# Normalising attention probabilities on GpSimd, with one reciprocal and one gate product per head

## The chip, the cores and the metric

One core of a Trainium2 chip runs the whole program in one launch. The metric is device microseconds, the median over several runs. The engines are named as in the profile: PE is TensorE (PEld its weight loads), DVE VectorE, ACT ScalarE, POOL GpSimd, SP the engine whose queue starts the transfers.

## The reference, cut to what matters

The reference is a decoder trunk of two layers on 512 tokens of width 1024. Each layer is a half-step SwiGLU, a mixer, and another half-step SwiGLU. The mixer projects the tokens into queries, keys and values, runs a pooling branch and an attention branch, and merges the two under gates. The part that the change touches is the softmax of two of the three attention branches and the gate that each is weighted with:

```python
def masked_softmax(s, mask):
    s = jnp.where(mask, s.astype(jnp.float32), -1e30)
    s = s - jnp.max(s, axis=-1, keepdims=True)
    p = jnp.where(mask, jnp.exp(s), 0.0)
    return p / jnp.maximum(jnp.sum(p, axis=-1, keepdims=True), 1e-30)
...
        return gc[..., 0:1] * o_cmp + gc[..., 1:2] * o_slc + gc[..., 2:3] * o_win
```

There are 16 heads of width 64 in two key groups. With 512 tokens the selected branch takes all blocks and the window spans the sequence, so both attend to every key up to the query.

## The kernel before

All activations stand transposed, features on the 128 partitions and the 512 tokens along the free axis. A float32 product is made of three passes over exact two-part splits of both operands (`mm3`, L114 to L116); each weight block is therefore split into `wh` on ACT (L107) and `wl` on DVE (L108) before PE can use it. Weights stream in through one queue (`load`, L92).

The program is a list of steps, but what the engines run is not in the order of the code: a scheduler places every instruction in its engine's queue, so that the products of one step stand between those of another. Each engine then works strictly through its own queue and waits by semaphores for the others.

In the attention stage of a layer, each of the 16 heads goes through two functions. `head_probs` makes, for each of four blocks of 128 queries (`qb`) and each of two branches (`br`), the scores on PE (L643 for the first two query blocks, L653 for the last two, in two banks `sc`), adds the distance and takes the minimum on DVE (L632, into a slot of `tbuf`; the scores are negated), takes the exponential and its row sum on ACT (L634, sums into the columns of `c`), and then on DVE inverts the sum (L658), multiplies it by the branch's gate (L659) and scales the block of probabilities by it (L662). A block of query `qb` has 128 (qb + 1) keys, so per head there are two blocks each of 128, 256, 384 and 512 columns. `head_out` of that head comes one step later in the code: it transposes the probabilities on PE (L675, 20 squares of 128 by 128 in six groups, three banks `pt`), splits each group into `ph` (ACT, L107) and `pl` (DVE, L108), and multiplies them with the values (L689, bank `pv`). The first group of a branch needs that branch's probabilities of all four query blocks.

Four times a layer `cmp_probs` makes the gated probabilities of the third branch for four heads; its scaling already runs on POOL (L605, tile `ec`). Between the heads stand the projections of the gates and of later queries (`ps_mm`, L114 to L116), which fill PE: `fill` in `mixer`. At the end of the mixer POOL also multiplies the pooling branch by its gate (L778, tile `bP`).

Of the kernel before, what the change touches and what calls it, by code (L numbers as in the profile page):

```python
# [14 lines left out]
ALU = mybir.AluOpType  # L15
# [3 lines left out]
T = 512  # L19
TB = T // P  # L20
# [9 lines left out]
MASKED = 1e30  # L30
# [21 lines left out]
class Trunk:  # L52
    """Activations are kept transposed: features on partitions, the 512 tokens
    along the free axis. A float32 product is three float32r passes over exact
    two-part splits of both operands (hi*hi + hi*lo + lo*hi)."""

# [10 lines left out]

# [1 line left out]
    def unit(self, tag, bufs, dt=F32, name=None, shape=(P, T)):  # L69
# [16 lines left out]

# [1 line left out]
    def load(self, src, kt, cols):  # L88
        """Rows (k p) of a [kt*128, cols] block onto partitions p."""
        raw = self.unit("wr", 3, F32, "wr", (P, 2048))  # L90
        v = raw[:, : kt * cols].rearrange("p (k c) -> p k c", k=kt)
        self.nc.sync.dma_start(v, src.rearrange("(k p) c -> p k c", p=P))  # L92
        return v

    def wsplit(self, v):
        """Exact split of a [128, a, b] weight block, a * b <= 1024."""
        a, b = v.shape[1], v.shape[2]
        out = []
        for nm in ("wh", "wl"):
            t = self.unit("w", 6, F32R, nm, (P, 1024))  # L100
            out.append(t[:, : a * b].rearrange("p (a b) -> p a b", a=a))
        hi, lo = out
        self.split(hi, lo, v)
        return hi, lo
# [5 lines left out]
    def mm3(self, out, terms, first=True, last=True):  # L110
        """out = sum over terms of lhsT^T rhs, each given as (lh, ll, rh, rl)."""
        n = len(terms)
        for i, (lh, ll, rh, rl) in enumerate(terms):
            self.nc.tensor.matmul(out, lh, rh, start=first and i == 0, stop=False)  # L114
            self.nc.tensor.matmul(out, lh, rl, start=False, stop=False)  # L115
            self.nc.tensor.matmul(out, ll, rh, start=False,  # L116
                                  stop=last and i == n - 1)

    def proj(self, tag, w, act):
        """One 128-feature output tile from a split weight unit."""  # L120
        out = self.bank(tag)
        hi, lo = w
        self.mm3(
            out,
            [(hi[:, k], lo[:, k], act[k][0], act[k][1]) for k in range(hi.shape[1])],
        )
        return out

# [1 line left out]
    def constants(self):  # L130
# [14 lines left out]
    def load_columns(self, names):  # L145
        """Per-feature vectors as columns, 128 features on partitions."""
        nc, io = self.nc, self.io
        rows = self.s("rows")[:, :P]
        r0 = min(ROWS[nm] for nm in names)
        n = 0  # L150
# [15 lines left out]
    def constants2(self):  # L166
        nc = self.nc

        def const(shape, name):
            return self.sb.tile(list(shape), F32, tag=name, name=name)  # L170

        # dist[p, c] = 384 + p - c, and MASKED where that is negative
        self.dist = const((P, T), "dist")
# [4 lines left out]
                                channel_multiplier=1)  # L178
        # distc[(j n), t] = t - (16 n + 31), and MASKED where that is negative
        self.distc = const((P, T), "distc")  # L180
        for j in range(4):
# [5 lines left out]
                                    channel_multiplier=-16)  # L187
        # qcol[(e d), m]: negated query scale over the slope of head 2 m + e
        self.qcol = const((P, ND), "qcol")
        for h in range(H):  # L190
            e = h % 2
            nc.gpsimd.memset(self.qcol[e * DH : e * DH + DH, h // 2 : h // 2 + 1],
                             -(DH ** -0.5) / SLOPES[h])
        # block[p, j] = 1 where p // 32 is j or j + 2
        self.block = const((P, 2), "block")
        nc.gpsimd.memset(self.block, 0.0)
        for j in range(4):
            nc.gpsimd.memset(self.block[32 * j : 32 * j + 32, j % 2 : j % 2 + 1], 1.0)
        # ramp[g, t] = w / (t + 1) for the first w tokens of pool group g
        self.ramp = const((P, 4, 16), "ramp")  # L200
# [4 lines left out]

# [1 line left out]
    def gain(self, x, col):  # L207
        """Split of x times its feature gain."""
        g = self.cols[:, col : col + 1]
        hi = self.unit("xg", 16, F32R, "xh")  # L210
        lo = self.unit("xg", 16, F32R, "xl")
        self.gained = (
            self.nc.scalar.activation(hi, x, AF.Copy, scale=g),
            self.nc.vector.scalar_tensor_tensor(lo, x, g, f32(hi), ALU.mult, ALU.subtract),
        )
        return hi, lo

    def norm_piece(self, d, x, row, split=True):
        """x[d] is final: gain it, split it, add its squares."""
        nc = self.nc  # L220
# [14 lines left out]
    def stats(self):  # L235
        """Per token 1/rms of the last normed activation, as columns per token
        block and (but after the last layer) along rows."""
        nc = self.nc
# [36 lines left out]

# [1 line left out]
    def run_steps(self, steps, nxt=0):  # L277
        """Steps are (fetch, run); each fetch is traced ahead of the run of the
        fetching step before it."""
        fetches = [i for i, (f, _) in enumerate(steps) if f]  # L280
        for i, (_, run) in enumerate(steps):
            while nxt < len(fetches) and (nxt == 0 or fetches[nxt - 1] <= i):
                steps[fetches[nxt]][0]()
                nxt += 1
            run()

    def units(self, src, n, kt, cols, cut, use, rows=False, pre=None):
        """Steps over n weight blocks [kt*128, cols], each cut into units of
        `cut` columns (or row tiles)."""
        steps = []  # L290
# [17 lines left out]

# [1 line left out]
    def ffn(self, wg, wu, wd, on_x):  # L310
# [41 lines left out]

# [1 line left out]
    def key_cmp_in(self, j, w):  # L354
        """Compressed-branch input as [(parity d), g, token pair]."""
        p = self.proj("mm", w, self.xg)
# [8 lines left out]
    def keys(self, br, w):  # L365
        """Keys stacked twice on partitions, hi and lo apart."""
        nc = self.nc
# [12 lines left out]
    def values(self, tb):  # L380
        """Values (stationary [keys, hi | lo]) and branch gates of a token block."""
        nc = self.nc
# [48 lines left out]
    def compress_steps(self, l, which):  # L431
        """MLP over the overlapping blocks of the compressed keys (which = 0) or
        values (1), the blocks stationary as [hi | lo]."""
        nc, io = self.nc, self.io
# [82 lines left out]

# [1 line left out]
    def pool_weights(self, l):  # L519
# [7 lines left out]
    def pool_unit(self, l, g, w):  # L527
        """Pool group g: trailing mean less the token, mixed and scaled."""
        nc = self.nc
# [28 lines left out]

# [1 line left out]
    def query_unit(self, m, w):  # L560
        """Per head of the pair the negated scaled query over the head's slope,
        [hi; lo] on partitions (odd heads [lo; hi])."""
        nc = self.nc
# [10 lines left out]
    def cmp_probs(self, qd):  # L574
        """Gated probabilities over the compressed keys of four heads, per head
        pair hi and lo stacked on partitions, [hi; lo] and [lo; hi]."""
        nc = self.nc
# [39 lines left out]
    def head_probs(self, h):  # L617
        """Gated probabilities of the selected and window branches, queries on
        partitions. The selection takes every block (8 of at most 16) and the
        window spans the sequence, so both attend to all keys up to the query."""  # L620
        nc = self.nc
# [15 lines left out]
        for qb in range(TB):  # L637
# [11 lines left out]
            else:  # L649
                for br in range(2):  # L650
# [5 lines left out]
                    probs[qb, br] = t  # L656
            ci = c[:, 2 * qb : 2 * qb + 2]
            nc.vector.reciprocal(ci, ci)  # L658
            nc.vector.tensor_mul(ci, ci, self.gates[:, qb, 3 * h + 1 : 3 * h + 3])  # L659
            for br in range(2):  # L660
                t = probs[qb, br]
                nc.vector.tensor_scalar(t, t, ci[:, br : br + 1], None, ALU.mult)  # L662

# [30 lines left out]

# [1 line left out]
    def mixer(self, l, on_x):  # L696
# [110 lines left out]

# [1 line left out]
    def run(self):  # L809
# [103 lines left out]
```

## Time and profile before

| | |
|---|---|
| median of 3 runs | 2415.21 us (2414.96 to 2421.27) |
| span of the profiled execution, first to last instruction | 2409.0 us |
| time outside the span, by the median | 6.2 us |
| busy: PE, DVE, ACT, POOL | 2377.3, 1398.9, 976.9, 51.5 us |
| attention stage of the first layer, of the second | about 490 to 765 us, 1655 to 1960 us |

The profile gives the span of its execution, not a device time of its own; the time outside the span is the difference to the median of the runs. A busy engine is not one at its peak: what a wait costs PE is read from the idle time of PE and PEld with what ended it, and from the distances between the starts of its products. In a row of grouped instructions, the form "out<-in xcount: min/median/max" or "busy us, mean ns" gives durations; "[idle before <-releaser]" in a timeline gives the wait ahead of a row.

### The profile page before, as it was taken

Reading aid. Unit: us, or ns where it says so; the run is one execution under the profiler, and the core shown is the slowest. Engines: PE = TensorE matmul, PEld = TensorE weight load, DVE = VectorE, ACT = ScalarE, POOL = GpSimd, SP = SyncE. Lnnn points to the kernel's source line nnn. Section 1 sums busy time; section 2 is a strip of 40 time slices with the busy share of each in tenths; the row PEclk is TensorE's granted clock in tenths of the full one; section 3 lists DMA queues with packets and bytes.
Section 4 is the critical chain, followed back from the end, with each engine's and each line's share of the span. In section 5 each row is a group of like instructions: output and inputs, shape, how many; then the busy total and the mean of one; then the engine's idle time right before and its main releaser. Section 6 shows DMA issues by size and latency. Waiting matters only on the chain.

```text
span 2409.0 us, 28552 instructions
## 1 busy us (share of the span) xinstructions
PE 2377.3 (99%) x11042; PEld 1951.9 (81%) x11042; DVE 1398.9 (58%) x2684; ACT 976.9 (41%) x1689; POOL 51.5 (2%) x106
## 2 busy tenths in 40 slices
PE   8999999999999999999999999999999999999998
PEld 6888888788888888888888888887888887888887
DVE  4434347778988544443544443567988975434444
ACT  4222234566666422222432222445666753222222
POOL 1000000000001000000000000000000010000000
PEclk9999999999999999999999999999999999999999
DMA  5332324422125422323232323335222253232321
GB/s 158 98 95 95 97 89 147 141 98 71 49 79 167 135 88 91 102 90 98 92 104 89 96 97 96 119 108 160 69 68 79 75 184 105 89 103 88 105 79 62
DMA packets 226007, 244.24 MB, mean 101 GB/s; under 512 B 8688, under 2 KB 206416, under 8 KB 225872
## 3 DMA queue, kind: packets, MB, share of 16 engines
q1 hardware_dynamic: 225696, 242.37, 31.6%
q8 instruction: 87, 1.43, 0.3%
q14 instruction: 48, 0.39, 0.1%
q10 hardware_dynamic: 176, 0.05, 0.0%
HBM read 223.53 MB, written 18.87 MB: 101 GB/s over the span
## 4 chain that ended last, share of the span: by engine, by line
PE 58%; issue 15%; DVE 1%; POOL 1%; DMA 1%; ACT 0%; POOLq 0%; DVEq 0%; SPq 0%; ACTq 0%
PE ps_mm L116 9%; PE ps_mm L115 9%; PE ps_mm L114 9%; PE ps_pv L689 4%; PE ps_sc L114 3%; PE ps_sc L115 3%; PE ps_sc L116 3%; PE ps_pt L114 3%; PE ps_pt L115 3%; PE ps_pt L116 3%; PE ps_pt L675 3%; PE ps_sc L653 2%; PE ps_sc L643 1%; DMA bP<-dB 1%; PE ps_sc L582 0%
## 5 line engine op out<-in xcount | busy, mean ns | idle before, releaser
L107 ACT ACTIVATE wh<-wr 128x1024 fp32r<-128x1024 f32 (+1 forms) x392 | 408.8, 1043 | 1099.5 <-PE ps_mm L115 414.3
L108 DVE TENSOR_TENSOR wl<-wr,wh 128x1024 fp32r<-128x1024 f32 (+1 forms) x392 | 469.9, 1200 | 76.6 <-ACT wh L107 75.5
L116 PE MATMUL ps_mm<-act,wl 128*128 128x512 f32 x704 | 280.8, 399 | 0.0
L114 PE MATMUL ps_sc<-xh,wh 128*128 128x512 f32 x704 | 277.1, 394 | 2.2 <-ACT x L838 2.2
L115 PE MATMUL ps_mm<-act,wh 128*128 128x512 f32 x704 | 277.6, 394 | 0.0
L114 PE MATMUL ps_mm<-act,wh 128*128 128x512 f32 x704 | 275.5, 392 | 0.0
L115 PE MATMUL ps_sc<-xl,wh 128*128 128x512 f32 x704 | 274.5, 390 | 0.0
L116 PE MATMUL ps_sc<-xh,wl 128*128 128x512 f32 x704 | 274.2, 389 | 0.0
L114 PE MATMUL ps_pt<-xh,wh 128*128 128x512 f32 x704 | 273.9, 389 | 0.0
L115 PE MATMUL ps_pt<-xl,wh 128*128 128x512 f32 x704 | 273.9, 389 | 0.0
L116 PE MATMUL ps_pt<-xh,wl 128*128 128x512 f32 x704 | 273.9, 389 | 0.0
L340 DVE SCALAR_TENSOR_TENSOR x<-ps_mm,x 128x512 f32<-128x512 f32 x96 | 66.4, 691 | 253.8 <-PE ps_mm L116 253.8
L331 DVE TENSOR_TENSOR u<-ps_pt,R 128x512 f32<-128x512 f32 x88 | 60.9, 692 | 245.7 <-PE ps_pt L116 245.7
L114 PE MATMUL ps_mm<-xh,wh 128*128 128x512 f32 x512 | 203.4, 397 | 0.0
L323 DVE TENSOR_TENSOR z<-ps_sc,R 128x512 f32<-128x512 f32 x88 | 60.9, 692 | 243.1 <-PE ps_sc L116 243.0
L116 PE MATMUL ps_mm<-xh,wl 128*128 128x512 f32 x512 | 200.9, 392 | 0.0
L115 PE MATMUL ps_mm<-xl,wh 128*128 128x512 f32 x512 | 200.8, 392 | 0.0
L115 PEld LDWEIGHTS ps_mm<-act,wh 128*128 128x128 f32 x704 | 132.1, 188 | 34.7 <-DVE act L108 0.8
L114 PEld LDWEIGHTS ps_sc<-xh,wh 128*128 128x128 f32 x704 | 132.4, 188 | 31.5 <-ACT x L838 2.6
L114 PEld LDWEIGHTS ps_mm<-act,wh 128*128 128x128 f32 x704 | 132.2, 188 | 31.6
L116 PEld LDWEIGHTS ps_mm<-act,wl 128*128 128x128 f32 x704 | 132.2, 188 | 30.5
L634 ACT ACTIVATE tbuf<-tbuf,m 128x128 f32<-128x128 f32 (+3 forms) x256 | 142.1, 556 | 36.3 <-DVE m L632 28.4
(238 smaller groups left out, 3864.6 us busy)
## 6 DMA issues: line engine op xcount, KB each, us to landing
wr<-in_ffn_w_gate_dram SPq DMA_DIRECT2D x44, 1024.0 KB, 5.4
wr<-in_ffn_w_up_dram SPq DMA_DIRECT2D x44, 1024.0 KB, 5.4
wr<-in_w_in_dram SPq DMA_DIRECT2D x34, 1024.0 KB, 5.3
wr<-in_ffn_w_down_dram SPq DMA_DIRECT2D x32, 1024.0 KB, 4.9
wr<-in_ffn_w_down_dram SPq DMA_DIRECT2D x16, 768.0 KB, 4.2
wr<-in_w_branch_nsa_dram SPq DMA_DIRECT2D x8, 1024.0 KB, 5.2
wr<-in_w_out_dram SPq DMA_DIRECT2D x8, 1024.0 KB, 5.3
dx<-x SPq DMA_DIRECT2D x16, 256.0 KB, 2.7
```

The source lines that it names most:

```text
L107: self.nc.scalar.activation(hi, src, AF.Copy)
L108: self.nc.vector.tensor_sub(lo, src, f32(hi))
L114: self.nc.tensor.matmul(out, lh, rh, start=first and i == 0, stop=False)
L115: self.nc.tensor.matmul(out, lh, rl, start=False, stop=False)
L116: self.nc.tensor.matmul(out, ll, rh, start=False, stop=last and i == n - 1)
L323: nc.vector.tensor_mul(z, g, self.R)
L331: nc.vector.tensor_mul(u, up, self.R)
L340: nc.vector.scalar_tensor_tensor(x, o, 0.5, x, ALU.mult, ALU.add)
L634: nc.scalar.activation(t, t, AF.Exp, scale=-1.0, bias=m[:, i : i + 1], accum_out=c[:, i : i + 1])
L653: nc.tensor.matmul(sp, qq, K[:, br, :nk], start=i == 0, stop=i == 1)
L675: nc.tensor.transpose(tp[:, w : w + P], probs[qb, br][:, kb * P : kb * P + P], self.ident)
L689: nc.tensor.matmul(out[:, T - n :], lhsT, rhs, start=i == 0, stop=i == len(ops) - 1)
```

## The change

The reciprocal and the product with the gates move out of the loop over query blocks: they run once per head over all eight columns of `c`, after the last exponential of the head. The eight scalings of a head move to POOL and follow that product.

```diff
@@ head_probs @@
                     softmax_num(t, sp, 2 * qb + br, nk)
                     probs[qb, br] = t
-            ci = c[:, 2 * qb : 2 * qb + 2]
-            nc.vector.reciprocal(ci, ci)
-            nc.vector.tensor_mul(ci, ci, self.gates[:, qb, 3 * h + 1 : 3 * h + 3])
+        nc.vector.reciprocal(c, c)
+        c3 = c.rearrange("p (b r) -> p b r", r=2)
+        nc.vector.tensor_mul(c3, c3, self.gates[:, :, 3 * h + 1 : 3 * h + 3])
+        for qb in range(TB):
             for br in range(2):
-                t = probs[qb, br]
-                nc.vector.tensor_scalar(t, t, ci[:, br : br + 1], None, ALU.mult)
+                t, i = probs[qb, br], 2 * qb + br
+                nc.gpsimd.tensor_scalar(t, t, c[:, i : i + 1], None, ALU.mult)
```

Comments and docstrings also go, and the lines from here on count one higher: the reciprocal is L657, the gate product L659, the scaling L663, the transposition L676, the product with the values L690. The scheduler places the attention stage anew.

DVE around the end of head 0 of a layer, the first of its 16 heads, before: the scores of the last query block (L632, 512 columns) stand among reciprocals, gate products and scalings of the earlier blocks.

```order
L632 ISA tbuf,m<-ps_sc,dist 128x512
L632 ISA m 128x1
L614 TENSOR_TENSOR pc<-ps_pt,pc 64x512
L662 TENSOR_SCALAR tbuf<-tbuf,c 128x256 x2
L658 RECIPROCAL c<-c 128x2
L632 ISA tbuf,m<-ps_sc,dist 128x512
L632 ISA m 128x1
L659 TENSOR_TENSOR c<-c,gates 128x2
L566 SCALAR_TENSOR_TENSOR qn<-ps_mm,qcol,R 128x512
L662 TENSOR_SCALAR tbuf<-tbuf,c 128x384 x2
```

The same place on DVE in the change, from the last scores of head 0 on.

```order
L632 ISA tbuf,m<-ps_sc,dist 128x512
L632 ISA m 128x1
L108 TENSOR_TENSOR wl<-wr,wh 128x1024
L614 TENSOR_TENSOR pc<-ps_pt,pc 64x512
L657 RECIPROCAL c<-c 128x8
L566 SCALAR_TENSOR_TENSOR qn<-ps_mm,qcol,R 128x512
L659 TENSOR_TENSOR c<-c,gates 128x8
```

The scalings are gone from DVE; the one gate product, for which all eight scalings of the head now wait, stands behind a weight split, a split of `pc` and a query product. In heads 2, 6 and 10 the same place reads as follows.

```order
L632 ISA tbuf,m<-ps_sc,dist 128x512
L632 ISA m 128x1
L108 TENSOR_TENSOR pl<-ps_pt,ph 128x384
L108 TENSOR_TENSOR wl<-wr,wh 128x1024
L657 RECIPROCAL c<-c 128x8
L108 TENSOR_TENSOR pl<-ps_pt,ph 128x512
L659 TENSOR_TENSOR c<-c,gates 128x8
```

PE where the first transpositions of head 0 stand, before: they begin after the first scores of head 1 (L643).

```order
L643 MATMUL ps_sc<-KH,q 128x256
L643 MATMUL ps_sc<-KL,q 128x256
L675 MATMUL ps_pt<-ident,tbuf 128x128 x2
L643 MATMUL ps_sc<-KH,q 128x512
L643 MATMUL ps_sc<-KL,q 128x512
L675 MATMUL ps_pt<-ident,tbuf 128x128
L114 MATMUL ps_mm<-xh,wh 128x512
L115 MATMUL ps_mm<-xl,wh 128x512
L116 MATMUL ps_mm<-xh,wl 128x512
L675 MATMUL ps_pt<-ident,tbuf 128x128 x3
```

The same place on PE in the change; between the last scores of head 0 and the first row stand 13 products of 512 columns.

```order
L643 MATMUL ps_sc<-KH,q 128x256
L643 MATMUL ps_sc<-KL,q 128x256
L643 MATMUL ps_sc<-KH,q 128x512
L643 MATMUL ps_sc<-KL,q 128x512
L114 MATMUL ps_mm<-xh,wh 128x512
L115 MATMUL ps_mm<-xl,wh 128x512
L116 MATMUL ps_mm<-xh,wl 128x512
L114 MATMUL ps_mm<-xh,wh 128x512
L676 MATMUL ps_pt<-ident,tbuf 128x128
L115 MATMUL ps_mm<-xl,wh 128x512
L653 MATMUL ps_sc<-KH,q 128x384
L653 MATMUL ps_sc<-KL,q 128x384
```

The next rows there are five transpositions, one product (L116) and four more transpositions. The first transposition of head 0 has moved behind six more rows of products; the first one, the second, the third and the seventh of the ten each wait for a scaling of their own (the first, third, fifth and seventh that POOL makes).

## Rows read from the trace of the kernel before

**Rows 1.** The page: its span, and the busy time of PE.

```profile
span 2409.0 us, 28552 instructions
PE 2377.3 (99%) x11042; PEld 1951.9 (81%) x11042; DVE 1398.9 (58%) x2684; ACT 976.9 (41%) x1689; POOL 51.5 (2%) x106
```

**Rows 2.** Busy time by window: first attention stage, and the feed-forward stage behind it.

```profile
490.00:765.00 275.00, 273.32 (x1450) 226.21 (x1451) 242.06 (x735) 183.16 (x447) 8.79 (x8) 1.00 0.25 80
1000.00:1275.00 275.00, 274.35 (x1202) 224.62 (x1202) 128.29 (x157) 82.72 (x103) 1.01 (x1) 1.00 0.30 94
```

**Rows 3.** Waits of PEld, whole span: waiter, releaser, us in total, times, longest.

```profile
PEld ps_pv L689 <- ACT ph L107: 7.6, 23, 0.8
PEld ps_pt L608 <- POOL ec L605: 4.9, 8, 0.7
...
PEld ps_pv L689 <- DVE pl L108: 2.2, 8, 0.4
```

**Rows 4.** The three lines that the change touches, whole span: duration min/median/max in ns.

```profile
L662 DVE TENSOR_SCALAR tbuf<-tbuf,c x256: 269/381/486, 506.7 to 1931.7; 128x128 f32<-128x128 f32 x32, 128x256 f32<-128x256 f32 x32, 128x384 f32<-128x384 f32 x32, 128x512 f32<-128x512 f32 x32
L658 DVE RECIPROCAL c<-c x128: 146/159/168, 505.1 to 1930.2; 128x2 f32<-128x2 f32 x128
L659 DVE TENSOR_TENSOR c<-c,gates x128: 141/155/525, 505.6 to 1930.8; 128x2 f32<-128x2 f32 x128
```

**Rows 5.** DVE groups by shape, first attention stage: busy us, mean ns, idle before.

```profile
L108 DVE TENSOR_TENSOR pl<-ps_pt,ph 128x384 fp32r<-128x384 f32 x64 | 34.4, 549 | 0.8 <-ACT ph L107 0.4
L108 DVE TENSOR_TENSOR wl<-wr,wh 128x1024 fp32r<-128x1024 f32 x25 | 30.2, 1215 | 6.2 <-ACT wh L107 6.1
L108 DVE TENSOR_TENSOR pl<-ps_pt,ph 128x512 fp32r<-128x512 f32 x32 | 21.9, 683 | 0.6 <-ACT ph L107 0.5
L632 DVE CUSTOM_DVE_ANT_0 tbuf<-ps_sc,dist 128x512 f32<-128x512 f32 x32 | 21.7, 678 | 0.2
...
L571 DVE TENSOR_TENSOR q<-qn,q 64x512 fp32r<-64x512 f32 x12 | 8.2, 686 | 0.4
...
L614 DVE TENSOR_TENSOR pc<-ps_pt,pc 64x512 fp32r<-64x512 f32 x8 | 5.5, 689 | 2.3 <-ACT pc L613 2.2
L566 DVE SCALAR_TENSOR_TENSOR qn<-ps_mm,qcol,R 128x512 f32<-128x512 f32 x6 | 4.5, 751 | 4.5 <-PE ps_mm L116 4.3
```

**Rows 6.** The timeline around POOL's first product of the attention stage.

```profile
504.66 0.17 DVE L604 TENSOR_TENSOR cc<-cc,gates 128x16 f32<-128x16 f32 x1
...
505.06 1.05 POOL L605 TENSOR_TENSOR ec<-ec,cc 128x512 f32<-128x512 f32 x1 [35.67 <-PE ps_sc L653]
...
505.63 0.50 DVE L659 TENSOR_TENSOR c<-c,gates 128x2 f32<-128x2 f32 x1
...
506.17 0.66 PE L608 MATMUL ps_pt<-ident,ec 128*128 128x128 f32 x4 [0.28 <-POOL ec L605]
```

**Rows 7.** POOL groups by shape, whole span: busy us, mean ns, idle before.

```profile
L176 POOL TENSOR_SCALAR_AFFINE_SELECT dist<-dist 128x512 f32<-128x512 f32 x1 | 0.6, 622 | 0.0
...
masks.py:199 POOL TENSOR_SCALAR_AFFINE_SELECT ident<-ident 128x128 f32<-128x128 f32 x1 | 0.3, 302 | 0.0
```

**Rows 8.** Timeline of PE: ten transpositions in a row.

```profile
678.77 1.25 PE L675 MATMUL ps_pt<-ident,tbuf 128*128 128x128 f32 x10
```

**Rows 9.** Separate waits in PE's queue at the transpositions, whole span: ns each.

```profile
L675 PEldq EVENT_SEMAPHORE  x74: 51/51/51, 517.8 to 1931.4; - x74
```

**Rows 10.** POOL and DVE side by side at the end of the attention stage.

```profile
752.39 1.30 POOL L778 TENSOR_TENSOR bP<-bP,sP 128x512 f32<-128x512 f32 x1 [51.36 <-ACT sP L777]
752.67 0.56 DVE L108 TENSOR_TENSOR pl<-ps_pt,ph 128x384 fp32r<-128x384 f32 x1 [0.25 <-ACT ph L107]
...
762.33 1.22 DVE L108 TENSOR_TENSOR wl<-wr,wh 128x1024 fp32r<-128x1024 f32 x1
762.35 2.35 POOL L778 TENSOR_TENSOR bP<-bP,sP 128x512 f32<-128x512 f32 x1 [8.66 <-ACT sP L777]
...
763.46 1.78 DVE L108 TENSOR_TENSOR ml<-sA,mh 128x512 fp32r<-128x512 f32 x1
```

## The prediction

> **What bounds the kernel now.** I read the page first. PE is busy 2377.3 of 2409.0 us [rows 1], so only what makes PE wait can move the end, whatever DVE and POOL save or spend. The windows come second: in the feed-forward stage PE issues 1202 products in 275 us, one of 512 columns every 0.229 us, with DVE busy for 128 us; in the attention stage DVE is busy for 242 of 275 us and POOL for under 9 [rows 2]. So DVE is the second bound of this one stage, and POOL is almost free there. The third view is the list of PE's waits. What the attention stage loses to late splits and probabilities is small: over both layers 7.6 us for `ph` (23 times, 0.33 each), 4.9 for `ec` from POOL and 2.2 for `pl` [rows 3]. That is all the change could win if every one of these waits went. No line of the list has PE wait for the scaling itself (L662): it is covered by the products that the scheduler puts between the last scores of a head and its first transposition.
>
> **The change part by part.**
>
> *Off DVE.* 256 scalings at 0.381 (97.5 us) and 96 of 128 reciprocals and gate products at 0.16 each (30 us) [rows 4]: some 128 us over 32 heads, 4 us a head, a quarter of DVE's time in this stage. None of it lies on the path, since DVE's lateness costs PE only through the waits just named. In the built order PE has 8 places where ten transpositions stand in a row, against 14 before; at such a place the product with `ph` often follows at once and waits. Six such places less, at 0.33 each [rows 3], give back 2.0 us. I count no more for the relief: other products with `ph` stand about as close behind their transpositions as before.
>
> *Onto POOL.* Eight scalings per head, in order of query block, both branches of each. PE needs the seventh of them before the first group of transpositions is complete. The first seven hold 2 x (128 + 256 + 384) + 512 = 2048 columns. No row shows a scaling on POOL. The nearest by kind, one tensor in and one out, is the masked select: 0.302 for 128 columns and 0.622 for 512, that is 0.195 fixed and 0.83 ns a column [rows 7], so 3.1 us for seven. From above stand its products of two operands: 1.05 for 512 columns with a broadcast operand [rows 6], so 4.2 us, and 1.30 with two full ones [rows 10], so 5.2 us. I take 3.1, since a scaling reads one tensor; the ends stay for the range. On the low side POOL could only come as quick as DVE, 0.28 to 0.48 an instruction [rows 4], 2.6 us.
>
> *The new wait, head 0.* All eight scalings wait for the head's single gate product, and that stands deep in DVE's queue. Count from the start of the last product of head 0's scores. DVE ends the minimum of the branch before at about 0.2, then a split of `pc` (0.69), the last minimum (0.68), the weight split (1.22), `pc` again (0.69), the reciprocal (0.16), `qn` (0.75), the gate product (0.16): 4.5 us [rows 4, 5]. POOL starts 0.23 after a product on DVE, and PE 0.06 after POOL [rows 6]. Seven scalings end at 4.8 + 3.1 = 7.9. PE comes there sooner: 14 products of 512 columns, two of 256, two of 512 and four more (4.8), then one transposition, one product, two of 384 columns, five transpositions and a product (1.6, at 0.125 a transposition [rows 8]): 6.4. It waits 1.5 us (1.0 at the low end, 2.6 and 3.6 at the upper ones). Before, the transpositions of head 0 stand early too, but PE waited little for them: the first blocks had been scaled one by one while the later scores ran. Twice, once a layer: 3.0 us. What is queued behind PE's wait is everything, so this time is lost; ACT and DVE only gain slack by it.
>
> *The new wait, other heads.* The next closest are heads 2, 6 and 10, and like them 15. There PE runs 24 products of 512 columns, four of 384, six of 256, four of 128 and six transpositions before the first transposition, by their columns 7.9 us, and reaches the fourth at 8.3. DVE ends the last minimum at about 1.4 (an estimate: product, minimum and a short queue), then `pl` (0.55), `wl` (1.22), reciprocal, `pl` (0.68), gate product: 4.2 [rows 5]. With the two hand-overs and 3.1 for POOL the scalings are there at 7.6: covered by 0.7 us. That cover goes if seven scalings take over 3.8; at 4.2 each of the 8 places costs 0.4, at 5.2 it costs 1.4. Other heads have 0.5 to 10 us more.
>
> *Waits as such.* PE's queue holds 24 separate wait instructions more in the built program (279 for 255), since a transposition now waits for POOL beside others. At 0.051 [rows 9] that is 1.2 us at most, none if they run ahead of the products; I take 1.2. DVE gets 210 more of them; against 128 us less work they don't count.
>
> *POOL beside DVE.* When `bP` met `wl` it took 2.35 us where another time it took 1.30, and `ml`, which reads two tensors in SBUF, took 1.78 where its like take 0.69; a tiny gate product beside `ec` took 0.50 for 0.155; yet `pl`, which reads PSUM, took its usual 0.56 beside `bP` [rows 4, 5, 6, 10]. So POOL and those DVE instructions that read two SBUF tensors take turns. The Trainium skill, GPSIMD Engine Reference, section 1 (Specifications), says the same: POOL shares its SBUF interfaces with DVE and contends with instructions of two SBUF inputs; whether a scaling with one tensor input is held too, no row here shows. Behind head 0's gate product stand two subtractions for `q` of 0.69 that read SBUF twice [rows 5]; they can hold the scalings by 0 to 1.4 us. I take half: 0.7, twice, 1.4 us. In heads 2, 6 and 10 `pl`, `o` and `z` follow, which read PSUM, so nothing holds POOL there. `wl` may be held by up to one scaling; weights are split several products ahead, so that is hidden.
>
> *The sum.* 3.0 + 1.4 + 1.2 - 2.0 = +3.6 us. The span becomes 2412.6; the median of the runs stands 6.2 above the profiled span, so 2418.8. A difference under 0.3% of the time (7.2 us) can't be told from no change here.
>
> **The rivals.**
>
> *POOL's scaling is slow.* At the price of products of two operands the waits come to 2 x 2.6 + 8 x 0.4 = 8.4 (4.2 us for seven) or 2 x 3.6 + 8 x 1.4 = 18.4 (5.2 us), with the other terms +9 to +19: 2424 to 2434. The point from which it decides is 3.8 us for seven scalings, where heads 2, 6, 10 and 15 lose their cover. For it: every POOL row with arithmetic on two tensors is at that price. Against: the select is not. The Trainium skill speaks for it in GPSIMD Engine Reference, section 4.1 (Engine selection): elementwise work belongs on VectorE, being about twice as slow on GpSimd with two inputs, though near line rate with one. By twice DVE's own time seven scalings would take 5.1 us, the slow end; by the best case of its section 3.1 (512 elements in 769 ns, an estimate of 3.1 us for 2048) the sum would stay.
>
> *DVE's relief counts in full.* If a quarter less work on DVE ends PE's waits for `ph` and `pl` altogether (9.8 us [rows 3]) and the scalings of head 0 come in time because DVE reaches the gate product with no queue ahead, the time falls by 9.8 less 1.2: 2406.6. It decides from 7.2 us net. For it: DVE is at 88% in this stage. Against: `ph` comes from ACT, whose work doesn't change, and 1 of the 23 waits is 0.8 long, so most are the bare latency from transposition to split.
>
> *Nothing reaches PE.* Head 0 is covered after all (POOL overtakes by 1.5 us, or earlier stalls delay PE as much), and the 2.0 and the 1.2 remain: 2414.4.
>
> **How the numbers follow.** The forecast case (waits at head 0, the rest covered) 0.52, from 2415 to 2423; POOL slow 0.28; DVE's relief 0.09; nothing reaches PE 0.11. The forecast is the likeliest case, 2418.8. A range of 2411 to 2434 leaves out about 2 in 10: most of the relief and the slowest end with contention on top. Faster by over 0.3% (under 2408): 0.08, the relief case nearly whole. Slower by over 0.3% (over 2422.5): the slow case and the upper edge of the forecast's, 0.34. No difference: 0.58.
>
> **What would show it.** The lines of POOL: 256 scalings at 0.30, 0.41, 0.52 and 0.62 us by shape. PE's waits: a line of transpositions that wait for POOL's `tbuf`, of about 3 to 4 us, almost all at the first head of each layer; many such waits, at a third of the heads or more, would mean the slow rival. DVE's busy time in the attention stage down by a quarter, with PE's wait for `ph` down from 7.6 to 5 or 6. DVE's own rows: `q` and `wl` longer than 0.69 and 1.22 beside POOL would show the turns. What would make the prediction wrong: a scaling that costs over 0.75 us at 512 columns, waits of `c` on ACT's last row sum that push the gate product later than 4.5 us, or a loss that isn't in PE's waits at all.

## The result, and the profile after

The change makes the kernel slower: 2471.4 us against 2415.1 us of the kernel before on the same chip, both medians of four runs, a ratio of 1.0231 with a 95% interval of 1.0205 to 1.0256. The prediction of 2418.8 us, range 2411 to 2434, is wrong. The loss is some 56 us, where +3.6 was forecast. Of all executions behind this document one is left out, one of the ten of the kernel by twos (below), which took 9928.5 us where its others took 2407.5 to 2418.3.

The page of the kernel after, its span and the busy time of each engine, answers to [rows 1]:

```profile
span 2465.9 us, 28742 instructions
PE 2400.0 (97%) x11042; PEld 1963.5 (80%) x11042; DVE 1317.4 (53%) x2236; ACT 971.6 (39%) x1689; POOL 333.6 (14%) x362
```

PE has as many instructions as before, and the span is 56.9 us longer, while PE is busy for only 22.7 us more. So most of the loss is PE standing still, and part of it is PE taking longer over the same work. DVE is busy for 81.5 us less; it brought nothing. (The prediction's 128 us added up durations, which in part overlap.)

The waits of PEld from 490 to 2000 us of the kernel after, which holds both attention stages (waiter, releaser, us in total, times, longest), answer to [rows 3]:

```profile
PEld ps_pt L676 <- POOL tbuf L663: 41.0, 24, 2.6
PEld ps_sc L653 <- issue: 5.4, 23, 0.3
PEld ps_pt L608 <- POOL ec L605: 5.0, 8, 0.9
PEld ps_pv L690 <- DVE pl L108: 4.4, 15, 0.4
...
PEld ps_pv L690 <- ACT ph L107: 4.3, 14, 0.4
```

The first line is new: the transpositions wait for POOL's scaling, 41.0 us in 24 waits, where the prediction had 3 to 4 us. The wait for `ph` fell from 7.6 to 4.3, and the one for `pl` rose from 2.2 to 4.4.

The groups of POOL by shape (busy us, mean ns, idle before) show why:

```profile
L663 POOL TENSOR_SCALAR tbuf<-tbuf,c 128x512 f32<-128x512 f32 x64 | 101.7, 1600 | 0.0
L663 POOL TENSOR_SCALAR tbuf<-tbuf,c 128x384 f32<-128x384 f32 x64 | 82.6, 1302 | 0.0
L663 POOL TENSOR_SCALAR tbuf<-tbuf,c 128x256 f32<-128x256 f32 x64 | 60.5, 957 | 0.0
L663 POOL TENSOR_SCALAR tbuf<-tbuf,c 128x128 f32<-128x128 f32 x64 | 39.7, 632 | 217.8 <-DVE c L659 163.2 <-ACT ph L107 42.4 <-ACT tbuf L634 12.3
```

A scaling of 512 columns takes 1.60 us on POOL, where DVE took 0.48 and the prediction put 0.62. By these means the first seven of a head take 2 x (0.632 + 0.957 + 1.302) + 1.600 = 7.4 us, not 3.1; in the timelines it is 7.0 at most heads and 7.7 at the first.

The timeline of PE at the first head (start, us, engine, line) shows the waits where the prediction put them, and how large they are:

```profile
512.76 0.33 PE L676 MATMUL ps_pt<-ident,tbuf 128*128 128x128 f32 x1 [0.47 <-POOL tbuf L663]
...
514.95 0.33 PE L676 MATMUL ps_pt<-ident,tbuf 128*128 128x128 f32 x1 [1.28 <-POOL tbuf L663]
517.07 1.11 PE L676 MATMUL ps_pt<-ident,tbuf 128*128 128x128 f32 x4 [1.79 <-POOL tbuf L663]
...
519.83 1.12 PE L676 MATMUL ps_pt<-ident,tbuf 128*128 128x128 f32 x4 [1.22 <-POOL tbuf L663]
```

Four waits come to 4.8 us. The last two groups of four transpositions take 1.1 us, where ten took 1.25 before [rows 8]. The windows (us of the stretch, busy time and count of PE, PEld, DVE, ACT and POOL, PE's granted clock, DMA share, GB/s) say what that is:

```profile
490.00:770.00 280.00, 263.97 (x1356) 215.01 (x1355) 188.08 (x494) 168.31 (x429) 140.64 (x130) 0.97 0.23 74
510.00:516.00 6.00, 3.53 (x16) 2.24 (x15) 4.87 (x17) 3.69 (x9) 3.91 (x5) 0.98 0.56 175
516.00:526.00 10.00, 7.71 (x25) 6.32 (x26) 2.96 (x7) 4.07 (x12) 5.32 (x4) 0.50 0.01 2
526.00:536.00 10.00, 10.00 (x53) 8.50 (x52) 6.04 (x12) 3.84 (x7) 7.32 (x7) 1.00 0.09 28
```

From 510 to 516 us PE is busy for 3.53 of 6 us. Then its granted clock is at 0.50, the lower of its two levels (1.2 of 2.4 GHz): 25 instructions in 10 us, where the next 10 us hold 53. So a wait can be paid a second time, where the work behind it runs at half the clock for a while. The clock records of this trace have eight such stretches in and just behind the two attention stages, 41.0 us in all, each begun within 3 us of a wait of PE for POOL of 1.2 to 2.4 us; the kernel before has none there. Not every such wait has one. Heads 2 and 6 of the first layer both wait 2.24 us, up to 554.85 and 624.76, and PE goes on with the same instructions; behind the second wait alone the clock is low:

```profile
554.80:558.20 3.40, 3.35 (x19) 2.81 (x20) 2.30 (x6) 1.40 (x4) 1.54 (x1) 1.00 0.00 0
624.90:628.30 3.40, 3.40 (x13) 3.13 (x13) 1.98 (x4) 1.31 (x3) 1.35 (x1) 0.51 0.00 0
```

### The profile page after: what moved, and what is told of

Read it like the earlier page. It is cut to its first block, busy times and chain, and to the rows that moved or that the text cites. A ratio compares the mean times of both kernels' runs of the same rounds, so it can differ in the third digit from the quotient of the medians.

```text
span 2465.9 us, 28742 instructions
## 1 busy us (share of the span) xinstructions
PE 2400.0 (97%) x11042; PEld 1963.5 (80%) x11042; DVE 1317.4 (53%) x2236; ACT 971.6 (39%) x1689; POOL 333.6 (14%) x362
## 4 chain that ended last, share of the span: by engine, by line
PE 72%; issue 17%; DVE 5%; POOL 4%; ACT 2%; DMA 0%; POOLq 0%; SPq 0%; DVEq 0%; ACTq 0%
PE ps_mm L114 12%; PE ps_mm L115 11%; PE ps_mm L116 11%; PE ps_sc L114 5%; PE ps_sc L115 5%; PE ps_sc L116 5%; PE ps_pt L114 5%; PE ps_pt L116 5%; PE ps_pt L115 5%; POOL tbuf L663 4%; PE ps_pv L690 2%; PE ps_pt L676 2%; PE ps_sc L653 1%; DVE wl L108 1%; DVE tbuf L632 1%
## 5 line engine op out<-in xcount | busy, mean ns | idle before, releaser
L663 POOL TENSOR_SCALAR tbuf<-tbuf,c 128x128 f32<-128x128 f32 (+3 forms) x256 | 282.2, 1123 | 217.8 <-DVE c L659 163.2
L116 PE MATMUL ps_mm<-act,wl 128*128 128x512 f32 x704 | 280.5, 398 | 0.0
L116 PE MATMUL ps_sc<-xh,wl 128*128 128x512 f32 x704 | 274.7, 390 | 0.0
L116 PE MATMUL ps_pt<-xh,wl 128*128 128x512 f32 x704 | 273.9, 389 | 0.0
L263 POOL TENSOR_TENSOR rcol<-v,mhalf 128x4 f32<-128x4 f32 x7 | 7.1, 1021 | 1567.7 <-DVE v L261 1567.7
L116 PE MATMUL ps_mm<-xh,wl 128*128 128x512 f32 x512 | 201.9, 394 | 0.0
```

The costliest lines, as they stand in the source:

```text
L116: self.nc.tensor.matmul(out, ll, rh, start=False, stop=last and i == n - 1)
L663: nc.gpsimd.tensor_scalar(t, t, c[:, i : i + 1], None, ALU.mult)
```

## The experiments

### One order, three prices

Two kernels keep every engine's instructions in the change's order, and put a cheaper instruction on POOL in place of the scaling. The first multiplies by the same column as a broadcast operand:

```diff
-                nc.gpsimd.tensor_scalar(t, t, c[:, i : i + 1], None, ALU.mult)
+                nc.gpsimd.tensor_mul(t, t, c[:, i : i + 1].broadcast_to([P, P * (qb + 1)]))
```

> The change with POOL's scaling written as a product of two tensors, the column of c broadcast, as ec is made (1.05 us for 512 columns against 1.60). Seven of them should take 4.2 to 4.7 us in place of 7.4. Theory A, by the prediction's formula (head 0 waits for the seven less 1.6 us, heads 2, 6, 10, 15 for the seven less 3.8): 2420 to 2430. Theory B: no change, 2465 to 2477. Theory C: a second operand from SBUF makes the turns worse, above 2470.

The second only copies the column over the block:

```diff
-                nc.gpsimd.tensor_scalar(t, t, c[:, i : i + 1], None, ALU.mult)
+                nc.gpsimd.tensor_copy(t, c[:, i : i + 1].broadcast_to([P, P * (qb + 1)]))
```

> The change, with a copy of the factor's column over the block on POOL in place of the scaling (the multiplication itself is left out); every engine has the same instructions in the same order as in the change, and a copy should take 0.3 to 0.6 us, that is some 3 us for the first seven. So with the change (7.4 us for seven) and the third experiment (5.0) it makes three prices in one and the same order. Theory A, only the price of seven scalings was mis-sized: the prediction's own sum holds, PE waits 2 to 5 us for `tbuf`, almost all at the first head of each layer, and the time is 0 to 7 us over before. Theory B, the order into which the scheduler puts the change's instructions loses some 12 us by itself, as the first, seventh and fifth experiments came out 11 to 18 us over before with hardly a wait for POOL: the waits for `tbuf` go, but the time stays 10 to 16 us over before.

The product: 2427.5 us, ratio 1.0066 (1.0049 to 1.0083). The copy: 2424.5 us, 1.0060 (1.0043 to 1.0077); its profiled execution took 2418.6, some 6 us under its median. The first seven take, by the mean of each shape, 2 x (0.411 + 0.644 + 0.857) + 1.132 = 4.96 us for the product, and 2 x (0.306 + 0.417 + 0.524) + 0.645 = 3.14 us for the copy, which is the prediction's price:

| first seven on POOL | ratio to before | PEld's wait for `tbuf` | lower clock in the attention stages |
|---|---|---|---|
| 3.14 us (copy) | 1.0060 | 5.1 us, 6 times | none |
| 4.96 us (product) | 1.0066 | 11.9 us, 10 times | 13.7 us |
| 7.4 us (the change) | 1.0231 | 41.0 us, 24 times | 41.0 us |

The lines of PEld's waits from 490 to 2000 us behind the first two rows of the table, the copy's first:

```profile
PEld ps_pt L676 <- POOL tbuf L663: 5.1, 6, 1.6
PEld ps_pt L676 <- POOL tbuf L663: 11.9, 10, 1.7
```

So some 40 of the 56 us are POOL's price: they go with nothing else changed. Copy and product are 9.3 us apart in their traces and hardly at all in their medians; what the copy's other executions lose is in no trace. Since the order is one, the place of the loss can be read too. Timeline of POOL at heads 10 and 11, of the change, of the product and of the copy (each row is a head's eight scalings in one):

```profile
689.70 8.52 POOL L663 TENSOR_SCALAR tbuf<-tbuf,c 128x128 f32<-128x128 f32 x8 [8.80 <-DVE c L659]
704.57 8.53 POOL L663 TENSOR_SCALAR tbuf<-tbuf,c 128x128 f32<-128x128 f32 x8 [6.34 <-ACT ph L107]
```

```profile
679.61 5.47 POOL L663 TENSOR_TENSOR tbuf<-tbuf,c 128x128 f32<-128x128 f32 x8 [11.76 <-DVE c L659]
691.10 5.48 POOL L663 TENSOR_TENSOR tbuf<-tbuf,c 128x128 f32<-128x128 f32 x8 [6.01 <-ACT ph L107]
```

```profile
675.62 3.24 POOL L663 COPY tbuf<-c 128x128 f32<-128x128 f32 x8 [14.97 <-DVE c L659]
687.11 3.24 POOL L663 COPY tbuf<-c 128x128 f32<-128x128 f32 x8 [8.24 <-ACT ph L107]
```

From head 10 to head 11 it is 11.49 us with the copy and with the product, and 14.87 with the scaling: 3.38 us lost at head 10, by the scaling alone. Taken so from the starts of every head's first POOL instruction, the change falls behind the copy by 6.6 and 5.7 us at the two first heads, by 2.3 to 4.3 at each of heads 2, 6 and 10 (with the head behind it), by some 7 about the last heads of each layer, and by nothing to speak of elsewhere; the product falls behind by 4.3 at each of the first heads alone. All six heads 2, 6 and 10 wait 2.2 to 2.3 us: the two with no stretch at the lower clock behind the wait lose 2.3, the four with one 4.2 to 4.3.

The slow rival's places are right, then, its deciding point is not: the product's seven cost nothing at heads 2, 6 and 10, though they take longer than 3.8 us (4.5 there, by the timeline). So it is luck that the prediction's formula gives the product's loss, 16 us at 4.96: 9 of these it puts on heads that paid nothing. PE's timeline of the change at head 10 gives the point:

```profile
696.74 0.90 PE L676 MATMUL ps_pt<-ident,tbuf 128*128 128x128 f32 x3 [2.27 <-POOL tbuf L663]
```

The chain that PE waits for there began with the 689.70 of the row above. Seven of its eight end by 8.52 - 1.60 = 6.9, less the wait of 2.27: some 4.7 us could have been hidden.

### Is it the form of the instruction?

The kernel before, with five POOL instructions on a 128x512 tile ahead of everything, twice:

```diff
...
+        for _ in range(2):
+            nc.gpsimd.tensor_scalar(r, a, k, None, ALU.mult)
+            nc.gpsimd.tensor_scalar(r, a, 1.5, None, ALU.mult)
+            nc.gpsimd.tensor_mul(r, a, k.broadcast_to([P, T]))
+            nc.gpsimd.tensor_copy(r, a)
+            nc.gpsimd.affine_select(out=r, in_=a, pattern=[[-1, T]], compare_op=ALU.is_ge,
+                                    fill=0.0, base=384, channel_multiplier=1)
```

> The kernel before, and ahead of all steps two rounds of five POOL instructions on an idle 128x512 tile: a scaling by a column (the form of the change), a scaling by a constant, a product with a broadcast column, a copy, and a masked select. Theory A, the column operand makes the scaling slow: the first takes 1.55 to 1.65 us, the scaling by a constant and the copy 0.6 to 0.8 like the select (0.62), the product 1.1. Theory B, arithmetic with a scalar is slow on POOL in either form: the scaling by a constant takes 1.5 us too, and the copy is at the select's price. Theory C, the change's scalings are slow because of where they stand (beside DVE, in place): on the idle tile the scaling by a column takes under 1 us.

The second of the two rounds in POOL's timeline:

```profile
31.04 1.56 POOL L855 TENSOR_SCALAR zr<-za,zk 128x512 f32<-128x512 f32 x1
32.69 2.50 POOL L856 TENSOR_SCALAR zr<-za 128x512 f32<-128x512 f32 x1
35.27 1.04 POOL L857 TENSOR_TENSOR zr<-za,zk 128x512 f32<-128x512 f32 x1
36.38 0.61 POOL L858 COPY zr<-za 128x512 f32<-128x512 f32 x1
37.06 0.61 POOL L859 TENSOR_SCALAR_AFFINE_SELECT zr<-za 128x512 f32<-128x512 f32 x1
```

Theory B holds. The scaling takes 1.56 us on an idle tile (1.59 in the first round), where it took 1.60 on the mean in the attention stage, so neither DVE nor its place there made it slow. A constant in place of the column doesn't help: 1.49 us in the first round, 2.50 in the second, where DVE's `wl` ran beside it from 32.61 to 33.84. The product with its two tensors is quicker (1.04; 1.62 in the first round, beside `wl` too), and only copy and select stand at the 0.61 that the prediction took for all three. The Trainium skill, GPSIMD Engine Reference, section 4.1 (Engine selection), has it the other way about: elementwise work with one input near line rate, with two inputs about half VectorE's speed. For a scaling the trace disagrees with the first half, 1.56 us against the 0.48 of DVE [rows 4], over three times as long.

### What stays with a cheap POOL

The copy still leaves some 14 us. Three kernels without POOL look for them. The first is the change with its scalings back on DVE:

```diff
-                nc.gpsimd.tensor_scalar(t, t, c[:, i : i + 1], None, ALU.mult)
+                nc.vector.tensor_scalar(t, t, c[:, i : i + 1], None, ALU.mult)
```

> One part of the change alone: one reciprocal and one gate product per head, the eight scalings stay on DVE. Theory A (the loss is the length of POOL's seven scalings, 7.4 us, between the head's gate product and PE's first group of transpositions, and the clock that falls while PE waits): with DVE's scalings the seven take 2.6 us, so the waits for tbuf go nearly all and the time is 2410 to 2420. Theory B (collecting the scalings behind one late gate product costs by itself, whichever engine scales): the time stays above 2440.

The second is the kernel before, reciprocal and gate product per query block, with the scalings written behind all four blocks:

```diff
+        for qb in range(TB):
             for br in range(2):
-                t = probs[qb, br]
-                nc.vector.tensor_scalar(t, t, ci[:, br : br + 1], None, ALU.mult)
+                t, i = probs[qb, br], 2 * qb + br
+                nc.vector.tensor_scalar(t, t, c[:, i : i + 1], None, ALU.mult)
```

> The kernel before, with reciprocal and gate product per query block as before, but the eight scalings of a head written behind all four blocks' gate products, on DVE: the same work, later. Theory A, the first experiment (one gate product per head, scaling on DVE, 15 us over before) lost because the scalings come late and in one row of eight on DVE: here the same 10 to 18 us. Theory A', it lost by the single gate product's wait for the last row sum: here under 5 us, since the first blocks' factors are there early. Theory B, any new order loses: 8 to 18 us, which can't be told from A by this run alone, but can by the one with pairs.

The third takes the query blocks by twos:

```diff
-            ci = c[:, 2 * qb : 2 * qb + 2]
-            nc.vector.reciprocal(ci, ci)
...
+            if qb % 2:
+                ci = c[:, 2 * qb - 2 : 2 * qb + 2]
+                nc.vector.reciprocal(ci, ci)
+                c3 = ci.rearrange("p (b r) -> p b r", r=2)
+                nc.vector.tensor_mul(c3, c3, self.gates[:, qb - 1 : qb + 1, 3 * h + 1 : 3 * h + 3])
+                for i in range(4):
+                    t = probs[qb - 1 + i // 2, i % 2]
+                    nc.vector.tensor_scalar(t, t, ci[:, i : i + 1], None, ALU.mult)
```

> The kernel before, with one reciprocal and one gate product per two query blocks, and the scalings on DVE behind them: DVE has 128 small instructions less, and POOL nothing more. Theory A, losses come only from POOL's price: as before, -4 to +4 us. Theory B, any new order that the scheduler makes of this stage loses by short waits for `ph`, `pl` and the issue: 8 to 18 us over before, as with one reciprocal and gate product per head on DVE.

Scalings back on DVE: 2427.9 us, 1.0064 (1.0043 to 1.0085). In its trace PE also ran at the lower clock for 10.2 us ahead of the stage's first scores, before there is any batch; but its shortest execution, 2424.9 us, is still 16.7 over the shortest of before. The same work as before, but late: 2424.2 us, 1.0054 (1.0037 to 1.0071). By twos: 2412.3 us, 1.0003 (0.9989 to 1.0016), though its order on PE is as far from before's as the others' are. So it is not that any new order loses. What the kernels that lose 13 to 16 us by their medians (9 to 20 by the intervals) have in common is that all eight scalings of a head come in one batch, behind its last scores; one gate product per head instead of four adds no more than a few us to it. The traces hold about half of this: the profiled executions of the late kernel and of the copy, both some 6 us under their medians, are 7.3 and 7.8 us longer in span than that of before. PE's waits of the late kernel, same view as above:

```profile
PEld ps_pv L690 <- ACT ph L107: 11.2, 26, 0.7
PEld ps_pv L690 <- DVE pl L108: 5.1, 23, 0.3
...
PEld ps_pt L676 <- DVE pc L614: 3.0, 4, 1.1
PEld ps_pt L676 <- DVE pl L108: 2.8, 12, 0.4
```

They are many short ones: `ph` 11.2 for the 7.6 of [rows 3], `pl` 5.1 for 2.2. The copy's trace has them in part (8.6 and 4.8), beside its 5.1 for `tbuf`. That the transpositions, released in one lump, crowd the products that need their splits is how I read these lines; it was not tried by itself.

### Which scaling comes first

The change, with the first branch's four blocks ahead of the second's:

```diff
-        for qb in range(TB):
-            for br in range(2):
+        for br in range(2):
+            for qb in range(TB):
```

> The change with POOL's eight scalings in another order: the four query blocks of the first branch, then those of the second. The first group of transpositions then needs four scalings (4.5 us) in place of seven (7.4). Theory A: the first group's waits fall by about 3 us at each place, some of it comes back at the second branch's first group, which needs all eight (9.1 us): 2430 to 2450. Theory B: 2465 to 2477.

2435.9 us, 1.0104 (1.0086 to 1.0122), with DVE's and ACT's order that of the change and PE's nearly so. PE's wait for `tbuf` falls from 41.0 to 16.4 us, as the first transpositions now need four scalings (4.6 us) and not seven. It is the sum ahead of the first transpositions that counts, not POOL's total, which hardly differs.

### POOL without the batch

Three kernels have reciprocal and gate product per query block, as before, and scale on POOL: in the change's form, as a product, and as a product for the second branch alone.

```diff
-                nc.vector.tensor_scalar(t, t, ci[:, br : br + 1], None, ALU.mult)
+                nc.gpsimd.tensor_scalar(t, t, ci[:, br : br + 1], None, ALU.mult)
```

> The other part alone: the scalings on POOL, but a reciprocal and a gate product per query block as before. Theory A: POOL scales the early blocks while later scores run, so only the last two blocks (3.2 us) stand behind the last gate product; most of the waits go and the time is 2413 to 2430. Theory C (POOL and DVE take turns at SBUF all through the stage, and that is what stretches POOL and delays both): the waits stay, above 2445.

```diff
-                nc.vector.tensor_scalar(t, t, ci[:, br : br + 1], None, ALU.mult)
+                nc.gpsimd.tensor_mul(t, t, ci[:, br : br + 1].broadcast_to([P, P * (qb + 1)]))
```

> The kernel before, with reciprocal and gate product per query block, and all scalings on POOL as products with a broadcast column. Against the second experiment (the same with the slow form of the scaling, 11 us over before) only the price differs. Theory A, the price of the form: the waits for POOL's `tbuf` fall from 5.5 to under 1 us, and the time to within 5 us of before. Theory B, the loss of the second experiment lies in the order and the waits for `pl` and the issue that came with it: the time stays 8 to 13 us over before.

```diff
-                nc.vector.tensor_scalar(t, t, ci[:, br : br + 1], None, ALU.mult)
+                if br:
+                    nc.gpsimd.tensor_mul(t, t, ci[:, 1:].broadcast_to([P, P * (qb + 1)]))
+                else:
+                    nc.vector.tensor_scalar(t, t, ci[:, :1], None, ALU.mult)
```

> The kernel before, with reciprocal and gate product per query block, and of each block's two scalings the second on POOL, as a product with a broadcast column; the first stays on DVE. Theory A (PE loses only by what it waits for POOL): a block's two scalings now run side by side, POOL's last one ends 1.13 us after its gate product where DVE's pair took 0.96, so no wait for `tbuf` of more than 1 us in all, DVE has some 49 us less to do, and the time is that of before within 6 us, possibly 2 to 6 us under it. Theory B (any hand-over to POOL in the middle of a head costs, as a re-placed order or as contention): 6 to 12 us over before.

2422.3 us, 1.0046 (1.0032 to 1.0060); 2423.4 us, 1.0055 (1.0038 to 1.0071); 2439.9 us, 1.0121 (1.0106 to 1.0136). With a scaling per block the slow form hurts no more than the quick one: three of a head's four blocks are scaled while later scores run. So price and batch make each other dearer: 11 us with the scalings on POOL alone, some 15 with the batch alone, 56 with both. The third kernel was meant as one that beats both, and is the worst of the three. DVE's and POOL's timeline at one head:

```profile
609.25 1.20 DVE L108 TENSOR_TENSOR wl<-wr,wh 128x1024 fp32r<-128x1024 f32 x1
...
609.42 1.71 POOL L663 TENSOR_TENSOR tbuf<-tbuf,c 128x384 f32<-128x384 f32 x1 [1.05 <-PE ps_mm L114]
...
610.37 0.98 DVE L665 TENSOR_SCALAR tbuf<-tbuf,c 128x384 f32<-128x384 f32 x1
...
611.59 1.04 POOL L663 TENSOR_TENSOR tbuf<-tbuf,c 128x512 f32<-128x512 f32 x1 [0.46 <-DVE c L659]
611.81 1.10 DVE L665 TENSOR_SCALAR tbuf<-tbuf,c 128x512 f32<-128x512 f32 x1
```

A scaling on DVE beside one on POOL takes 0.98 and 1.10 us, where the mean of its shape before was 0.41 and 0.48 (over the whole run the two shapes now take 0.84 and 1.02 on the mean), and POOL's first, which has `wl` beside it too, takes 1.71 for the 0.86 of the product in the change's order: a pair side by side takes no less than two in a row on DVE. DVE's busy time falls by 1.4 us, to 1397.5, where I had expected 49. How much of its 30 us is that, and how much its order, stays open, as does what the other two lose: their waits for `pl` are 10.1 us in 42 and 14.9 in 48, without a row that says why.

### Half of the columns

The change with POOL's product over every second column; half of the scaling is left out:

```diff
-                nc.gpsimd.tensor_scalar(t, t, c[:, i : i + 1], None, ALU.mult)
+                t = t[:, ::2]
+                nc.gpsimd.tensor_mul(t, t, c[:, i : i + 1].broadcast_to([P, P * (qb + 1) // 2]))
```

> This kernel is the change with POOL's scaling as a product with a broadcast column, over every second column only: half of the scaling is left out, so that POOL's price comes near the one that the prediction took. By the rows of the third experiment (0.41, 0.64, 0.86 and 1.13 us for 128 to 512 columns) the first seven should take about 3.1 us. Theory A, only the price of seven scalings was mis-sized: PE waits for POOL's `tbuf` at the first heads of the layers alone, 2 to 5 us in all, and the time comes within some 8 us of before, 2411 to 2421 beside a before of 2411 to 2415. Theory B, one gate product per head costs by itself, whatever the scaling takes: as with the scaling on DVE, 12 us or more over before, 2424 or more, with PE's waits for `ph` or for the issue up.

2427.8 us, 1.0074 (1.0059 to 1.0089), with 6.5 us of waits for `tbuf`. It spoke for theory B; but in eight places PE's order is another than the change's, so the copy is the cleaner run at this price.

## Why the prediction was wrong

**The step that failed** is the size of one term: "I take 3.1, since a scaling reads one tensor". Seven scalings took 7.4 us, beyond the upper end of 5.2 that I had drawn from products of two operands, so the range could not hold the time either. The number of tensors read does not order POOL's instructions: copy and select 0.61, product 1.04 to 1.13, scaling 1.56 to 1.60 us for 512 columns. A masked select and a scaling are alike only in their operands.

**The chain** was right. The gate product stood where I counted it: it ends 4.6 us behind the start of the last product of head 0's scores, for the 4.5 of the prediction.

```profile
507.29 0.40 PE L653 MATMUL ps_sc<-KL,q 128*128 128x512 f32 x1
...
511.75 0.16 DVE L659 TENSOR_TENSOR c<-c,gates 128x8 f32<-128x8 f32 x1
```

The hand-overs were about as said, the losses fell on the first heads and on heads 2, 6, 10 and 15 of each layer, and the prediction's own formula, with 7.4 for 3.1, gives 2 x 5.8 = 11.6 us for the first heads and 8 x 3.6 = 28.8 for the eight others, 40.4 in all; the waits for `tbuf` are 41.0. That the two agree so well is partly luck: the eight waited for 21.9 us, with a cover of 4.7 us and not 3.8, and heads 12, 13 and 14, which the formula leaves out, for 6.7.

**The clock** is a cost that the sum lacked. Behind most of the longer waits PE is granted the lower of its levels. In 41.0 us of such stretches it does the work of half that time where it is not waiting; with PE busy for 7.7 of 10 us in the longest, as the windows show, that is some 15 us, an estimate from these rows. The copy's trace, with the same instructions in the same order and no such stretch, bears it out: waits left out, they take 14.9 us less there. With the waits that makes about the 56, so that the short waits that the batch brings elsewhere hardly show in the change. That PE, late already, finds its splits ready is how I read this; the wait for `ph`, 4.3 us for the copy's 8.6, fits it.

**The turns of POOL and DVE** were sized well: eight scalings take 8.52 us at head 10 and 9.24 at head 0, where the subtractions stand: 0.7 us, the value taken.

```profile
512.09 9.24 POOL L663 TENSOR_SCALAR tbuf<-tbuf,c 128x128 f32<-128x128 f32 x8 [6.68 <-DVE c L659]
```

**The relief** was wrong in sign at the forecast's own price. I counted -2.0 for fewer transpositions in a row. The copy, which pays 3.14 us for seven and waits 5.1 us for `tbuf` (predicted, with the turns, 4.4), should have come out at about +3.6; it came at 1.0060. The batch makes the short waits for `ph` and `pl` more, not fewer, as the late kernel on DVE shows. In the change itself `ph` did fall, to 4.3, beside the long waits for `tbuf`. So at 3.1 the forecast would still have been some 10 us too low by the medians, 4 by the copy's trace.

**The rivals.** The slow one was right in kind, and the measured price lay above its 5.2. DVE's relief in full is refuted: DVE is busy for 83 us less in the copy as well, a sixth and not a quarter of its time in the two attention stages, and nothing was won. The half of the Trainium skill's rule that spoke for my 3.1, one input near line rate (GPSIMD Engine Reference, section 4.1), is the half that the trace does not keep for a scaling.

## What to carry to other kernels

Price an operation on another engine by the same operation there, or by the slowest neighbour, not by one that reads as many tensors; and where no row has it, let the range reach past every neighbour. What counts is the time from the last input to the first consumer: eight small jobs made one batch behind the last of their inputs cost 13 to 16 us by the medians here even on the old engine, while batches of half the size cost nothing that can be told. And where an engine's clock falls behind a wait, as it did here behind most of the longer ones, a wait costs more than its length.

## What was not expected of the hardware

- A scaling by a column or a constant on POOL takes 1.5 us and more for 512 columns, a product of two tensors 1.04, a copy or a select 0.61.
- A scaling on DVE (one tensor in SBUF to SBUF) that runs beside a product on POOL takes 0.98 us at 384 columns, for 0.41 alone (0.84 on the mean of 32); the product 1.71, for 0.86, with a weight split beside it as well.
- PE's granted clock was at 0.50 for 10 us behind waits of 0.5, 1.3 and 1.8 us, and for 3.4 us or 6.8 behind six of eight single waits of 2.2 to 2.4 us, but not behind the other two; the work in these stretches took up to twice its time.
